# A column mean over 8192 x 8192: reordering the last six tiles and splitting them differently between VectorE and TensorE

## Chip, cores, metric

The kernel runs on one core of one Trainium2 chip. The metric is device time in microseconds (us), lower is better. "Span" is the time from the first to the last instruction in the profile; it is about 2 us shorter than the time of the same run.

Names used below: PE is TensorE, DVE is VectorE, ACT is ScalarE, SP is SyncE. SP and ACT only issue DMAs here, except for two small copies on ACT at the end. "Tile t" is rows 128t to 128t+127 of the input (128 x 8192 floats, 4 MB). "Block b" is columns 512b to 512b+511. The two DMA queues are also called rings. A load has "landed" when its data are in the buffer. The "granted clock" is the share of PE's full clock that it was given.

## The reference

```python
def setup_inputs():
    return {"x": np.random.randn(8192, 8192).astype(np.float32)}

def reference(x):
    return np.mean(x, axis=0)
```

The kernel reads 268 MB and writes 32 KB. So it cannot be faster than the input can be loaded.

## The kernel before

64 tiles come in over two DMA queues (even tiles from SP, odd ones from ACT) into four buffers (tile 0 goes straight into `acc`). DVE adds each tile to an accumulator `acc` of 128 x 8192. At the end PE sums over the 128 partitions: a matmul of one block with a 128 x 16 matrix, whose only nonzero column holds 1/8192, adds the block's column sums to one row of a PSUM tile. `psA` holds blocks 0 to 13, `psB` blocks 14 and 15. Since such a matmul accumulates, PE can also take a block of a tile directly, without DVE. The text calls such blocks "raw".

```python
    def mm(src, b, ps, row, start, stop):
        nc.tensor.matmul(out=ps[:], lhsT=w16[:, 16 - row : 32 - row],
            rhs=src[:, b * BLK : (b + 1) * BLK], start=start, stop=stop)
    # ... mmA: a row of psA; mmB: a row of psB; raws(src): blocks 13, 14, 15 of src

    for t0 in range(0, 56, 2):
        # ... load tiles t0 and t0+1 whole, one on each queue; DVE adds 8192 columns of each

    for t0 in (56, 58, 60):
        # ... load both tiles whole; at 56: mmA(acc, 13), mmB(acc, 14), mmB(acc, 15)
        # DVE adds columns 0:6656 (blocks 0 to 12) of each; then raws() of each

    dve_units = [(g * 1024, (g + 1) * 1024) for g in range(5)] + [
        (b * BLK, (b + 1) * BLK) for b in (10, 11, 12)
    ]
    # ... tile 62 on SP: raw columns first, then dve_units
    for c0, c1 in dve_units:                       # tile 63 on ACT: raw blocks LAST
        nc.scalar.dma_start(out=pbuf[63][:, c0:c1], in_=x[63 * P : 64 * P, c0:c1])
    for b in PE_B:                                 # (13, 14, 15)
        c0, c1 = b * BLK, (b + 1) * BLK
        nc.scalar.dma_start(out=pbuf[63][:, c0:c1], in_=x[63 * P : 64 * P, c0:c1])

    raws(pbuf[62])
    done_blk = 0
    for c0, c1 in dve_units:
        order = (63, 62) if c1 - c0 == 1024 else (62, 63)
        for t in order:
            nc.vector.tensor_add(out=acc[:, c0:c1], in0=acc[:, c0:c1], in1=pbuf[t][:, c0:c1])
        while (done_blk + 1) * BLK <= c1:
            mmA(acc, done_blk)
            done_blk += 1
    mmA(pbuf[63], 13, stop=True)
    mmB(pbuf[63], 14)
    mmB(pbuf[63], 15, stop=True)
    # ... ACT copies psA and psB to SBUF, two DMAs write the output
```

The order of instructions on PE is not the order of the text here; a scheduler sets it when the program is built. In the trace of this kernel the two `psB` matmuls of tile 63, last in the text, start at 626.14 us, ahead of the 13 matmuls of sums, which run from 629.4 on.

Of the kernel before, what the change touches and what calls it, by code (L numbers as in the profile page):

```python
# [1 line left out]

# [4 lines left out]


@with_exitstack
def kernel(  # L10
    ctx: ExitStack,
    tc: tile.TileContext,
    x: bass.AP,
    out: bass.AP,
):
    nc = tc.nc
    P = nc.NUM_PARTITIONS
    R, C = x.shape
    assert R % P == 0
    n_tiles = R // P  # L20
    fp32 = mybir.dt.float32

    BLK = 512
    n_blk = C // BLK
    assert n_blk <= 16 and C % BLK == 0

    special = n_tiles == 64 and C == 8192
    N_STREAM_BUFS = 4

    acc_pool = ctx.enter_context(tc.tile_pool(name="acc", bufs=1))  # L30
    acc = acc_pool.tile([P, C], fp32, tag="acc", name="acc")

    const_pool = ctx.enter_context(tc.tile_pool(name="const", bufs=1))
    w16 = const_pool.tile([P, 48], fp32, tag="w16", name="w16")
    res = const_pool.tile([16, BLK], fp32, tag="res", name="res")
    res2 = const_pool.tile([2, BLK], fp32, tag="res2", name="res2")

    stream_pool = ctx.enter_context(tc.tile_pool(name="stream", bufs=N_STREAM_BUFS))

    psum_pool = ctx.enter_context(tc.tile_pool(name="psum", bufs=1, space=bass.MemoryType.PSUM))  # L40
    psA = psum_pool.tile([16, BLK], fp32, tag="psA", name="psA")
    psB = psum_pool.tile([16, BLK], fp32, tag="psB", name="psB")

    rings = [nc.sync, nc.scalar]
    out2d = out.rearrange("(a b) -> a b", b=BLK)

    rings[0].dma_start(out=acc[:], in_=x[0:P, :])  # L47
    nc.vector.memset(w16[:], 0.0)  # L48
    nc.vector.memset(w16[:, 16:17], 1.0 / R)  # L49

    def mm(src, b, ps, row, start, stop):
        nc.tensor.matmul(  # L52
            out=ps[:],
            lhsT=w16[:, 16 - row : 32 - row],
            rhs=src[:, b * BLK : (b + 1) * BLK],
            start=start,
            stop=stop,
        )

    if not special:  # L60
        for t0 in range(0, n_tiles, 2):
            pair = [t for t in (t0, t0 + 1) if 0 < t < n_tiles]
            bufs = {}
            for t in pair:
                bufs[t] = stream_pool.tile([P, C], fp32, tag="xt", name=f"x_t{t}")
                rings[t % 2].dma_start(out=bufs[t][:], in_=x[t * P : (t + 1) * P, :])
            for t in pair:
                nc.vector.tensor_add(out=acc[:], in0=acc[:], in1=bufs[t][:])
        for b in range(n_blk):
            mm(acc, b, psA, row=b, start=(b == 0), stop=(b == n_blk - 1))  # L70
        nc.scalar.copy(out=res[:n_blk], in_=psA[:n_blk])
        nc.scalar.dma_start(out=out2d, in_=res[:n_blk])
        return

    PE_B = (13, 14, 15)
    D1 = PE_B[0] * BLK

    psA_started = [False]
    psB_started = [False]

    def mmA(src, b, stop=False):
        mm(src, b, psA, row=b, start=not psA_started[0], stop=stop)
        psA_started[0] = True

    def mmB(src, b, stop=False):
        mm(src, b, psB, row=b - 14, start=not psB_started[0], stop=stop)
        psB_started[0] = True

    def raws(src, stop=False):
        mmA(src, 13)  # L90
        mmB(src, 14)
        mmB(src, 15, stop=stop)

    for t0 in range(0, 56, 2):
        pair = [t for t in (t0, t0 + 1) if t > 0]
        bufs = {}
        for t in pair:
            bufs[t] = stream_pool.tile([P, C], fp32, tag="xt", name=f"x_t{t}")
            rings[t % 2].dma_start(out=bufs[t][:], in_=x[t * P : (t + 1) * P, :])
        for t in pair:  # L100
            nc.vector.tensor_add(out=acc[:], in0=acc[:], in1=bufs[t][:])  # L101

    for t0 in (56, 58, 60):
        bufs = {}
        for t in (t0, t0 + 1):
            bufs[t] = stream_pool.tile([P, C], fp32, tag="xt", name=f"x_t{t}")
            rings[t % 2].dma_start(out=bufs[t][:], in_=x[t * P : (t + 1) * P, :])  # L107
        if t0 == 56:
            mmA(acc, 13)
            mmB(acc, 14)  # L110
            mmB(acc, 15)
        for t in (t0, t0 + 1):
            nc.vector.tensor_add(  # L113
                out=acc[:, 0:D1], in0=acc[:, 0:D1], in1=bufs[t][:, 0:D1]
            )
        for t in (t0, t0 + 1):
            raws(bufs[t])

    dve_units = [(g * 1024, (g + 1) * 1024) for g in range(5)] + [
        (b * BLK, (b + 1) * BLK) for b in (10, 11, 12)  # L120
    ]
    pbuf = {}
    for t in (62, 63):
        pbuf[t] = stream_pool.tile([P, C], fp32, tag="xt", name=f"x_t{t}")
    nc.sync.dma_start(out=pbuf[62][:, D1:C], in_=x[62 * P : 63 * P, D1:C])
    for c0, c1 in dve_units:
        nc.sync.dma_start(out=pbuf[62][:, c0:c1], in_=x[62 * P : 63 * P, c0:c1])
    for c0, c1 in dve_units:
        nc.scalar.dma_start(out=pbuf[63][:, c0:c1], in_=x[63 * P : 64 * P, c0:c1])  # L129
    for b in PE_B:  # L130
        c0, c1 = b * BLK, (b + 1) * BLK
        nc.scalar.dma_start(out=pbuf[63][:, c0:c1], in_=x[63 * P : 64 * P, c0:c1])  # L132

    raws(pbuf[62])

    done_blk = 0
    for c0, c1 in dve_units:
        order = (63, 62) if c1 - c0 == 1024 else (62, 63)
        for t in order:
            nc.vector.tensor_add(  # L140
                out=acc[:, c0:c1], in0=acc[:, c0:c1], in1=pbuf[t][:, c0:c1]
            )
        while (done_blk + 1) * BLK <= c1:
            mmA(acc, done_blk)
            done_blk += 1
    assert done_blk == 13

    mmA(pbuf[63], 13, stop=True)
    mmB(pbuf[63], 14)
    mmB(pbuf[63], 15, stop=True)  # L150

    nc.scalar.copy(out=res[0:14], in_=psA[0:14])  # L152
    nc.sync.dma_start(out=out2d[0:14], in_=res[0:14])
    nc.scalar.copy(out=res2[0:2], in_=psB[0:2])  # L154
    nc.scalar.dma_start(out=out2d[14:16], in_=res2[0:2])


# [1 line left out]
_INS = ['x']  # L159
_OUTS = [((8192,), 'float32')]  # L160


# [23 lines left out]
```

## Time and profile before

| what | before |
|---|---|
| time, median of 13 runs | 647.78 us (647.07 to 648.64) |
| span of the profiled run | 645.4 us |
| HBM rate over the span | 416 GB/s |
| DVE busy | 83% |
| PE busy | 7% |

The part of the page that cuts the span into 40 slices of 16.1 us, kernel before. The digits are busy tenths; PEclk is the granted PE clock in tenths of full speed.

```profile
DVE  0538998888898888898888998888998888987693
...
PEclk9999999999999999999999999999999999997669
DMA  9999999999999999999999999999999999999970
GB/s 390 422 433 445 422 422 443 435 422 433 445 422 424 443 433 422 433 445 422 425 441 433 424 433 441 424 426 441 433 424 435 439 424 424 443 433 425 411 304 2
```

DMA is full from start to slice 38. DVE follows it, at about nine tenths. There is nothing to win in the first 600 us except a faster DMA. What can be won is the end: the last slice has an almost empty DMA, and the one before it is down to 304 GB/s.

Two windows of the same trace. The columns are: busy us (and instructions) of PE, PEld, DVE, ACT, POOL; granted clock; DMA share; GB/s.

```profile
120.00:480.00 360.00, 0.00 (x0) 0.00 (x0) 322.52 (x38) 0.00 (x0) 0.00 (x0) 1.00 1.00 432
610.00:620.00 10.00, 4.71 (x11) 0.87 (x9) 9.93 (x3) 0.00 (x0) 0.00 (x0) 0.95 1.03 405
```

In the steady part the tiles come in rows of 32 KB at 432 GB/s. From 606 us on they come in pieces with rows of 2 to 6 KB, at 405 GB/s between 610 and 620 us.

The end of the chain of waits, which is the work that ended last, followed back from step to step to what released it (start us, duration us, what):

```profile
619.55 6.55 DMA x_t<-in_x_dram
...
626.14 3.46 PE psB L52 x4
629.60 12.03 PE psA L52 x28
...
641.66 0.57 ACT res L152
```

The last of tile 63 lands at 626.1 to 626.7 us (semaphore events of the trace). Then PE multiplies for 15.5 us, 16 matmuls, before the copy and the output. Each matmul is two instructions in this trace (the reason why "x28" is 14 matmuls), 0.43 us apart each at full clock: 0.86 us per block. The granted clock was 0.50 from 619.1 to 629.3 us here, and the instructions issued in that time were 0.85 us apart; that is why 16 matmuls took 15.5 us and not 16 x 0.86 = 13.8.

DVE in the same stretch (timeline; in brackets the idle time before, and what ended it; a line with several adds is named after the first, so "x16" is ten adds of 1024 columns and six of 512):

```profile
585.43 14.22 DVE L113 TENSOR_TENSOR acc<-acc,x_t 128x6656 f32<-128x6656 f32 x2 [5.21 <-DMA x_t<-in_x_dram]
604.87 14.22 DVE L113 TENSOR_TENSOR acc<-acc,x_t 128x6656 f32<-128x6656 f32 x2 [5.22 <-DMA x_t<-in_x_dram]
619.12 15.05 DVE L140 TENSOR_TENSOR acc<-acc,x_t 128x1024 f32<-128x1024 f32 x16
```

DVE has no gap from 604.87 to 634.17. So two things end late: PE at 641.63, because its queue waited for the last landing, and DVE at 634.2, 8 us after the last data.

### The profile page before, as it was taken

The numbers are of one execution on the slowest core, as the hardware profiler recorded it, in microseconds if no ns is written. First come the engines' busy times: TensorE is split into PE (matmuls) and PEld (weight loads), VectorE is DVE, ScalarE is ACT, GpSimd is POOL, SyncE is SP. The second block draws the span as 40 slices with busy tenths as digits, with TensorE's granted clock in tenths as the row PEclk, the third lists the DMA queues.
The fourth block names the chain that finished last, engine by engine and source line by source line (L and its number), as shares of the span: only waits on it lengthen the run. The fifth ranks groups of instructions, "written<-read, shape, count | busy, mean of one in ns | idle before, by whom it ended". The sixth has DMA issues, their size and how long they took to land.

```text
span 645.4 us, 503 instructions
## 1 busy us (share of the span) xinstructions
PE 42.0 (7%) x80; PEld 8.2 (1%) x80; DVE 535.8 (83%) x79; ACT 2.4 (0%) x3; POOL 0.2 (0%) x4
## 2 busy tenths in 40 slices
PE   0000000000000000000000000000000000054527
PEld 0000000000000000000000000000000000010101
DVE  0538998888898888898888998888998888987693
ACT  0000000000000000000000000000000000000000
POOL 0000000000000000000000000000000000000000
PEclk9999999999999999999999999999999999997669
DMA  9999999999999999999999999999999999999970
GB/s 390 422 433 445 422 422 443 435 422 433 445 422 424 443 433 422 433 445 422 425 441 433 424 433 441 424 426 441 433 424 435 439 424 424 443 433 425 411 304 2
DMA packets 11842, 268.49 MB, mean 416 GB/s; under 512 B 1328, under 2 KB 1328, under 8 KB 3904
## 3 DMA queue, kind: packets, MB, share of 16 engines
q1 hardware_dynamic: 5788, 134.25, 48.5%
q10 hardware_dynamic: 6052, 134.22, 48.5%
q14 instruction: 2, 0.02, 0.0%
HBM read 268.44 MB, written 0.03 MB: 416 GB/s over the span
## 4 chain that ended last, share of the span: by engine, by line
DMA 74%; DVE 22%; PE 2%; another core or an unknown queue 0%; issue 0%; ACTq 0%; ACT 0%; SPq 0%; DVEq 0%
DMA x_t<-in_x_dram 74%; DVE acc L101 20%; DVE acc L113 2%; PE psA L52 2%; PE psB L52 1%; ACTq L129 0%; ACT res L152 0%; ACTq L132 0%; SPq L47 0%; DVEq L101 0%; ACTq L107 0%; DVEq L113 0%
## 5 line engine op out<-in xcount | busy, mean ns | idle before, releaser
L101 DVE TENSOR_TENSOR acc<-acc,x_t 128x8192 f32<-128x8192 f32 x55 | 478.1, 8692 | 84.9 <-DMA x_t<-in_x_dram 84.0
L113 DVE TENSOR_TENSOR acc<-acc,x_t 128x6656 f32<-128x6656 f32 x6 | 42.6, 7092 | 12.6 <-DMA x_t<-in_x_dram 12.4
L52 PE MATMUL psA<-acc,w 128*16 128x512 f32 x28 | 13.2, 625 | 564.0 <-DVE acc L101 564.0
L52 PE MATMUL psB<-x_t,w 128*16 128x512 f32 x32 | 18.5, 708 | 11.4 <-DMA x_t<-in_x_dram 11.4
L140 DVE TENSOR_TENSOR acc<-acc,x_t 128x1024 f32<-128x1024 f32 (+1 forms) x16 | 15.1, 1019 | 0.0
L52 PE MATMUL psA<-x_t,w 128*16 128x512 f32 x16 | 9.9, 706 | 24.2 <-DMA x_t<-in_x_dram 24.2
L52 PEld LDWEIGHTS psA<-acc,w 128*16 128x16 f32 x28 | 2.7, 100 | 573.3 <-DVE acc L101 564.0
L52 PEld LDWEIGHTS psB<-x_t,w 128*16 128x16 f32 x32 | 3.5, 112 | 25.8 <-DMA x_t<-in_x_dram 13.1
L154 ACT ACT_TABLE_LOAD x1 | 1.3, 1283 | 621.8 <-DMA x_t<-in_x_dram 621.8
L52 PE MATMUL psB<-acc,w 128*16 128x512 f32 x4 | 3.0, 887 | 0.0
L52 PEld LDWEIGHTS psA<-x_t,w 128*16 128x16 f32 x16 | 1.4, 99 | 30.5 <-DMA x_t<-in_x_dram 26.0
L48 DVE MEMSET w<- 128x48 f32 x1 | 0.1, 98 | 0.8 <-PEq L170 0.8
L52 PEld LDWEIGHTS psB<-acc,w 128*16 128x16 f32 x4 | 0.6, 151 | 2.8 <-issue 2.8
L152 ACT COPY res<-psA 14x512 f32<-14x512 f32 x1 | 0.6, 574 | 11.4 <-PE psA L52 11.4
L154 ACT COPY res<-psB 2x512 f32<-2x512 f32 x1 | 0.6, 574 | 6.5 <-PE psB L52 6.5
L49 DVE MEMSET w<- 128x1 f32 x1 | 0.1, 59 | 0.1
L170 POOL MEMSET const-bfloat16-1.0<- 128x1 bf16 x1 | 0.1, 101 | 0.0
L170 POOL MEMSET const-uint8-127<- 128x1 uint8 x1 | 0.1, 101 | 0.0
L170 POOL MEMSET const-float32-0.0<- 128x1 f32 x1 | 0.1, 98 | 0.2 <-issue 0.2
L170 POOL MEMSET const-float32-1.0<- 128x1 f32 x1 | 0.1, 98 | 0.0
## 6 DMA issues: line engine op xcount, KB each, us to landing
x_t<-in_x_dram ACTq DMA_DIRECT2D x31, 4096.0 KB, 24.5
x_t<-in_x_dram SPq DMA_DIRECT2D x30, 4096.0 KB, 30.1
acc<-in_x_dram SPq DMA_DIRECT2D x1, 4096.0 KB, 21.7
x_t<-in_x_dram SPq DMA_DIRECT2D x5, 512.0 KB, 19.1
x_t<-in_x_dram ACTq DMA_DIRECT2D x5, 512.0 KB, 6.7
x_t<-in_x_dram ACTq DMA_DIRECT2D x6, 256.0 KB, 6.2
x_t<-in_x_dram SPq DMA_DIRECT2D x1, 768.0 KB, 16.4
x_t<-in_x_dram SPq DMA_DIRECT2D x3, 256.0 KB, 6.8
```

What stands on the lines that cost most here:

```text
L48: nc.vector.memset(w16[:], 0.0)
L49: nc.vector.memset(w16[:, 16:17], 1.0 / R)
L52: nc.tensor.matmul(out=ps[:], lhsT=w16[:, 16 - row : 32 - row], rhs=src[:, b * BLK : (b + 1) * BLK], start=start, stop=stop,)
L101: nc.vector.tensor_add(out=acc[:], in0=acc[:], in1=bufs[t][:])
L113: nc.vector.tensor_add(out=acc[:, 0:D1], in0=acc[:, 0:D1], in1=bufs[t][:, 0:D1])
L140: nc.vector.tensor_add(out=acc[:, c0:c1], in0=acc[:, c0:c1], in1=pbuf[t][:, c0:c1])
L152: nc.scalar.copy(out=res[0:14], in_=psA[0:14])
L154: nc.scalar.copy(out=res2[0:2], in_=psB[0:2])
L170: nc = _bacc.Bacc("TRN2", target_bir_lowering=False, num_devices=1)
```

## The change

It means to shorten the end. PE's instruction order is pinned to the text (`manual_schedule`). The raw blocks of tiles 62 and 63 are loaded and multiplied first, so that after the last add only a matmul of a summed block is left. PE takes six raw blocks instead of three of tiles 58 to 61. Tiles 60 and 61 come in pieces. The core of the diff, with cuts:

```diff
-    for t0 in range(0, 56, 2):
+    for t0 in range(0, 58, 2):                 # two more full tiles for DVE
 ...
-    for t0 in (56, 58, 60):
-        ... whole loads; DVE columns 0:6656, PE blocks 13, 14, 15
+    with tc.manual_schedule(engines={mybir.EngineType.PE}):
+        mmB(acc, 14)
+        mmB(acc, 15)
+        PE_LO = 10
+        D1 = PE_LO * BLK
+        ... tiles 58, 59: whole loads; DVE columns 0:5120, PE blocks 10 to 15
+        dve_units_a = [(g * 1024, (g + 1) * 1024) for g in range(5)]
+        for t in (60, 61):
+            bufs[t] = new_buf(t)
+            rings[t % 2].dma_start(out=bufs[t][:, D1:C], in_=x[t * P : (t + 1) * P, D1:C])
+            for c0, c1 in dve_units_a:
+                rings[t % 2].dma_start(
+                    out=bufs[t][:, c0:c1], in_=x[t * P : (t + 1) * P, c0:c1])
+        ... DVE adds the five units of 60 and 61, PE blocks 10 to 15
-    ... tile 62: raw first; tile 63: raw last; psA of sums, then psA, psB, psB of tile 63
+        raw_units = [(7168, 8192)]
+        tail_units = dve_units_a + [(5120, 6144), (6144, 6656), (6656, 7168)]
+        for c0, c1 in raw_units + tail_units:
+            for t in (62, 63):
+                rings[t % 2].dma_start(
+                    out=bufs[t][:, c0:c1], in_=x[t * P : (t + 1) * P, c0:c1])
+        for c0, c1 in raw_units:
+            for t in (62, 63):
+                for b in range(c0 // BLK, c1 // BLK):
+                    mm_raw(bufs[t], b, stop=(t == 63 and b == 15))
+        for c0, c1 in tail_units:
+            for t in (62, 63):
+                nc.vector.tensor_add(
+                    out=acc[:, c0:c1], in0=acc[:, c0:c1], in1=bufs[t][:, c0:c1])
+            for b in range(c0 // BLK, c1 // BLK):
+                mmA(acc, b, stop=(c1 == tail_units[-1][1] and b == c1 // BLK - 1))
```

More of the change, by code (lines that the diff above doesn't have):

```diff
@@ L58, in mm, with new_buf @@
         )
+    def new_buf(t):
+        return stream_pool.tile([P, C], fp32, tag="xt", name=f"x_t{t}")
     if not special:
@@ L64 @@
             for t in pair:
-                bufs[t] = stream_pool.tile([P, C], fp32, tag="xt", name=f"x_t{t}")
+                bufs[t] = new_buf(t)
                 rings[t % 2].dma_start(out=bufs[t][:], in_=x[t * P : (t + 1) * P, :])
@@ L73 @@
         return
-    PE_B = (13, 14, 15)
-    D1 = PE_B[0] * BLK
     psA_started = [False]
@@ L87, in mmB, with mm_raw @@
         psB_started[0] = True
-    def raws(src, stop=False):
-        mmA(src, 13)
-        mmB(src, 14)
-        mmB(src, 15, stop=stop)
-    for t0 in range(0, 56, 2):
+    def mm_raw(src, b, stop=False):
+        if b >= 14:
+            mmB(src, b, stop=stop)
+        else:
+            mmA(src, b, stop=stop)
+    bufs = {}
+    for t0 in range(0, 58, 2):
         pair = [t for t in (t0, t0 + 1) if t > 0]
-        bufs = {}
         for t in pair:
-            bufs[t] = stream_pool.tile([P, C], fp32, tag="xt", name=f"x_t{t}")
+            bufs[t] = new_buf(t)
             rings[t % 2].dma_start(out=bufs[t][:], in_=x[t * P : (t + 1) * P, :])
@@ L101 @@
             nc.vector.tensor_add(out=acc[:], in0=acc[:], in1=bufs[t][:])
-    for t0 in (56, 58, 60):
-        bufs = {}
-        for t in (t0, t0 + 1):
-            bufs[t] = stream_pool.tile([P, C], fp32, tag="xt", name=f"x_t{t}")
-            rings[t % 2].dma_start(out=bufs[t][:], in_=x[t * P : (t + 1) * P, :])
-        if t0 == 56:
-            mmA(acc, 13)
-            mmB(acc, 14)
-            mmB(acc, 15)
-        for t in (t0, t0 + 1):
-            nc.vector.tensor_add(
-                out=acc[:, 0:D1], in0=acc[:, 0:D1], in1=bufs[t][:, 0:D1]
-            )
-        for t in (t0, t0 + 1):
-            raws(bufs[t])
@@ L119 @@
-    dve_units = [(g * 1024, (g + 1) * 1024) for g in range(5)] + [
-        (b * BLK, (b + 1) * BLK) for b in (10, 11, 12)
-    ]
-    pbuf = {}
-    for t in (62, 63):
-        pbuf[t] = stream_pool.tile([P, C], fp32, tag="xt", name=f"x_t{t}")
-    nc.sync.dma_start(out=pbuf[62][:, D1:C], in_=x[62 * P : 63 * P, D1:C])
-    for c0, c1 in dve_units:
-        nc.sync.dma_start(out=pbuf[62][:, c0:c1], in_=x[62 * P : 63 * P, c0:c1])
-    for c0, c1 in dve_units:
-        nc.scalar.dma_start(out=pbuf[63][:, c0:c1], in_=x[63 * P : 64 * P, c0:c1])
@@ L130 @@
-    for b in PE_B:
-        c0, c1 = b * BLK, (b + 1) * BLK
-        nc.scalar.dma_start(out=pbuf[63][:, c0:c1], in_=x[63 * P : 64 * P, c0:c1])
-    raws(pbuf[62])
-    done_blk = 0
-    for c0, c1 in dve_units:
-        order = (63, 62) if c1 - c0 == 1024 else (62, 63)
-        for t in order:
-            nc.vector.tensor_add(
-                out=acc[:, c0:c1], in0=acc[:, c0:c1], in1=pbuf[t][:, c0:c1]
-            )
-        while (done_blk + 1) * BLK <= c1:
-            mmA(acc, done_blk)
-            done_blk += 1
@@ L146 @@
-    assert done_blk == 13
-    mmA(pbuf[63], 13, stop=True)
-    mmB(pbuf[63], 14)
-    mmB(pbuf[63], 15, stop=True)
-    nc.scalar.copy(out=res[0:14], in_=psA[0:14])
-    nc.sync.dma_start(out=out2d[0:14], in_=res[0:14])
-    nc.scalar.copy(out=res2[0:2], in_=psB[0:2])
-    nc.scalar.dma_start(out=out2d[14:16], in_=res2[0:2])
+    with tc.manual_schedule(engines={mybir.EngineType.PE}):
[3 more added lines that the diff above has]
+        D1 = PE_LO * BLK
+        for t in (58, 59):
+            bufs[t] = new_buf(t)
+            rings[t % 2].dma_start(out=bufs[t][:], in_=x[t * P : (t + 1) * P, :])
+        for t in (58, 59):
+            nc.vector.tensor_add(out=acc[:, 0:D1], in0=acc[:, 0:D1], in1=bufs[t][:, 0:D1])
+        for t in (58, 59):
+            for b in range(PE_LO, 16):
+                mm_raw(bufs[t], b)
+        dve_units_a = [(g * 1024, (g + 1) * 1024) for g in range(5)]
+        for t in (60, 61):
+            bufs[t] = new_buf(t)
+            rings[t % 2].dma_start(out=bufs[t][:, D1:C], in_=x[t * P : (t + 1) * P, D1:C])
+            for c0, c1 in dve_units_a:
+                rings[t % 2].dma_start(
+                    out=bufs[t][:, c0:c1], in_=x[t * P : (t + 1) * P, c0:c1]
+                )
+        for c0, c1 in dve_units_a:
+            for t in (60, 61):
+                nc.vector.tensor_add(
+                    out=acc[:, c0:c1], in0=acc[:, c0:c1], in1=bufs[t][:, c0:c1]
+                )
+        for t in (60, 61):
+            for b in range(PE_LO, 16):
+                mm_raw(bufs[t], b)
+        raw_units = [(7168, 8192)]
+        tail_units = dve_units_a + [(5120, 6144), (6144, 6656), (6656, 7168)]
+        for t in (62, 63):
+            bufs[t] = new_buf(t)
+        for c0, c1 in raw_units + tail_units:
+            for t in (62, 63):
+                rings[t % 2].dma_start(
+                    out=bufs[t][:, c0:c1], in_=x[t * P : (t + 1) * P, c0:c1]
+                )
+        for c0, c1 in raw_units:
[3 more added lines that the diff above has]
+        for c0, c1 in tail_units:
+            for t in (62, 63):
+                nc.vector.tensor_add(
+                    out=acc[:, c0:c1], in0=acc[:, c0:c1], in1=bufs[t][:, c0:c1]
+                )
+            for b in range(c0 // BLK, c1 // BLK):
+                mmA(acc, b, stop=(c1 == tail_units[-1][1] and b == c1 // BLK - 1))
+        nc.scalar.copy(out=res2[0:2], in_=psB[0:2])
+        nc.scalar.dma_start(out=out2d[14:16], in_=res2[0:2])
+        nc.scalar.copy(out=res[0:14], in_=psA[0:14])
+        nc.sync.dma_start(out=out2d[0:14], in_=res[0:14])
```

## The prediction

> **What bounds it now.** The page: DMA is nine tenths busy or more in nearly every slice; 416 GB/s over a 645.4 us span. The chain of waits repeats every 38.85 us per four tiles (16.8 MB, 432 GB/s); DVE adds take 8.69 us per 128x8192 tile, 17.4 of every 19.4 us. So up to about 605 us DMA binds, and the change leaves that alone. The last pieces of tile 63 land at 626.1 to 626.7. What follows is a 19 us tail.
>
> In the chain, PE starts psB at 626.14 (3.46 us), then psA (12.03 us), to 641.63; the psA copy (0.57 us) and the output DMA end the span 3.8 us later. PE's instruction order has tile 63's two psB matmuls ahead of all psA matmuls of finished blocks. They wait for the last landings, and 13 psA matmuls that could have started near 622 queue behind. DVE ends at 634.2, without a gap from 604.87 (2 x 7.09 us for tiles 60, 61, then 15.05 us).
>
> **What the change does.**
> - PE order pinned, raw blocks of 62/63 loaded and multiplied first: psA matmuls run as units finish, one matmul remains after the last add. Removes up to 12 us of tail.
> - Six blocks instead of three go to PE for tiles 58 to 61: DVE saves 4 x 1.6 us (8.69 less 7.09, per 1536 columns); tiles 56, 57 become full adds (+2 x 1.6), tiles 62/63 have one block more (+1.0). PE gets some 10 us more work, off the chain.
> - Tiles 60, 61 come in pieces, so their adds start near 596 instead of 605. This relieves DVE at the end.
> - Cost: 4 KB rows move at 405 GB/s against 432 (table of windows); 5.2 MB more of them is about 0.8 us. More DMAs wait for an earlier one's semaphore; two rings with work queued should hide that.
> - DVE's order has tile 62's first unit before tile 61's last, so DVE idles till about 610.
>
> **Estimate.** Laying landings (432/405 GB/s, two rings sharing) and adds (1.13 us per 1024 columns, 0.63 per 512) side by side: last landing 626.5 to 627.3, hardly changed; DVE then has two units of backlog and ends near 629; the last four matmuls take 0.86 us each at full clock, so PE ends near 630.7 against 641.63. 647.5 - 10.9 = 636.6 us, 1.7% less. Even with only one add and one matmul after the last landing it would be near 633.
>
> **Clock.** [...] granted 0.50 until 608.9, then 1.00. At half clock a matmul is 1.71 us. I expect PE busy without a break from about 608 to 618[...]; half clock there would add 3.5 us.
>
> Predicted 636.5 us, 8 in 10 between 633.0 and 640.5. Faster by over 2%: 0.22; within 2%: 0.77; slower by over 2%: 0.01.
>
> **What would show it.** Right: last landing within 1 us of 626.5; last add near 629; chain ending DMA, DVE adds, one to four psA matmuls, copy; psB copy long before; slices up to 36 as before. Wrong: more than 4 matmuls piled up after the last add; DVE ending after 631; last landing after 628.
>
> **What would make it wrong.** A dry ring (issues held by semaphores) in 600 to 626, delaying the last landing; DVE's fixed order stalling on late units; half clock at the end. Faster if the smaller pieces overlap better and DVE keeps pace.

Full clock for the last four matmuls was the assumption. 641.63 - 630.7 = 10.9, and 647.5 - 10.9 = 636.6 us, with the four matmuls at the 0.86 us each that the trace shows at granted clock 1.00. "Half clock there" means at the last four matmuls: 4 x (1.71 - 0.86) = 3.4 us by these figures. The waits for "an earlier one's semaphore" are those of the trace before: of the 14 loads issued from 600 us on, 10 were issued 0.02 to 0.05 us after the earlier DMA on the same semaphore had landed. That two rings would hide more of them was an estimate.

## The result

| | before | after |
|---|---|---|
| median, runs | 647.78 us, 13 | 637.82 us, 8 |
| range | 647.07 to 648.64 | 637.64 to 638.1 |
| span of the profiled run | 645.4 | 635.9 |
| last landing | 626.7 | 627.5 |
| last add of DVE ends | 634.2 | 630.6 |
| last matmul of PE ends | 641.6 | 632.3 |
| mean granted PE clock | 0.974 | 0.999 |

The ratio is 0.9844 (95% interval 0.9834 to 0.9853): 10 us, 1.6%.

The slices after, of 15.9 us each:

```profile
DVE  0538998888988888988889888899888898888966
...
PEclk9999999999999999999999999999999999999999
DMA  9999999999999999999999999999999999999994
GB/s 385 439 429 429 429 429 429 429 433 437 439 437 431 429 429 429 429 429 429 435 437 435 437 431 429 429 429 429 429 429 437 437 435 437 431 429 416 410 409 156
```

Up to slice 36 DMA and DVE are about as busy as before. The end of the chain of waits after:

```profile
611.94 7.99 DMA x_t<-in_x_dram
...
620.02 2.44 DVE acc L151 x3
...
623.43 0.98 DVE acc L151
...
624.57 1.77 DVE acc L151 x2
...
627.44 1.23 DVE acc L151
...
628.72 3.62 PE psA L52 x8
...
632.36 0.57 ACT res L158
```

Where before showed 15.5 us of matmuls after the last landing, there are now adds up to 630.6 us and the last eight PE instructions (four matmuls, 3.6 us). DVE's timeline after:

```profile
585.64 11.02 DVE L114 TENSOR_TENSOR acc<-acc,x_t 128x5120 f32<-128x5120 f32 x2 [2.01 <-DMA x_t<-in_x_dram]
596.69 1.22 DVE L129 TENSOR_TENSOR acc<-acc,x_t 128x1024 f32<-128x1024 f32 x1
...
603.18 2.36 DVE L129 TENSOR_TENSOR acc<-acc,x_t 128x1024 f32<-128x1024 f32 x2 [0.19 <-DMA x_t<-in_x_dram]
607.52 2.36 DVE L129 TENSOR_TENSOR acc<-acc,x_t 128x1024 f32<-128x1024 f32 x2 [1.98 <-DMA x_t<-in_x_dram]
...
614.90 4.63 DVE L151 TENSOR_TENSOR acc<-acc,x_t 128x1024 f32<-128x1024 f32 x4 [2.75 <-DMA x_t<-in_x_dram]
620.02 10.57 DVE L151 TENSOR_TENSOR acc<-acc,x_t 128x1024 f32<-128x1024 f32 x11 [0.49 <-DMA x_t<-in_x_dram]
```

DVE starts on tile 60 at 596.7, not at 604.9. Yet it then waits for landings, about 5 us in all between 600 and 615, and it still ends 3 us after the last landing. The two windows after:

```profile
120.00:480.00 360.00, 0.00 (x0) 0.00 (x0) 322.31 (x38) 0.00 (x0) 0.00 (x0) 1.00 1.00 432
610.00:620.00 10.00, 4.19 (x9) 0.72 (x10) 6.78 (x6) 0.00 (x0) 0.00 (x0) 1.00 1.02 409
```

The steady part is the same to the digit. At the end it is 409 GB/s in 4 KB rows.

### The profile page after: what moved, and what is told of

The parts are those of the page before. It is cut to its first block, busy times and chain, and to the rows that moved or that the text cites. A ratio compares the mean times of both kernels' runs of the same rounds, so it can differ in the third digit from the quotient of the medians.

```text
span 635.9 us, 537 instructions
## 1 busy us (share of the span) xinstructions
PE 40.5 (6%) x88; PEld 8.1 (1%) x88; DVE 534.6 (84%) x87; ACT 2.4 (0%) x3; POOL 0.2 (0%) x4
## 4 chain that ended last, share of the span: by engine, by line
DMA 78%; DVE 20%; issue 1%; PE 1%; ACT 0%; SPq 0%; DVEq 0%
DMA x_t<-in_x_dram 78%; DVE acc L102 19%; DVE acc L151 1%; PE psA L52 1%; ACT res L158 0%; SPq L47 0%; DVEq L102 0%; DVEq L151 0%
## 5 line engine op out<-in xcount | busy, mean ns | idle before, releaser
L102 DVE TENSOR_TENSOR acc<-acc,x_t 128x8192 f32<-128x8192 f32 x57 | 495.5, 8692 | 87.1 <-DMA x_t<-in_x_dram 64.5
L151 DVE TENSOR_TENSOR acc<-acc,x_t 128x1024 f32<-128x1024 f32 (+1 forms) x16 | 16.4, 1087 | 3.3 <-DMA x_t<-in_x_dram 3.2
L52 PE MATMUL psA<-x_t,w 128*16 128x512 f32 x32 | 14.4, 592 | 0.0
L129 DVE TENSOR_TENSOR acc<-acc,x_t 128x1024 f32<-128x1024 f32 x10 | 11.8, 1222 | 2.6 <-DMA x_t<-in_x_dram 2.6
L114 DVE TENSOR_TENSOR acc<-acc,x_t 128x5120 f32<-128x5120 f32 x2 | 11.0, 5491 | 2.0 <-DMA x_t<-in_x_dram 2.0
L52 PE MATMUL psB<-x_t,w 128*16 128x512 f32 x24 | 11.1, 593 | 2.8 <-DMA x_t<-in_x_dram 2.8
L156 ACT ACT_TABLE_LOAD x1 | 1.3, 1283 | 622.6 <-DMA x_t<-in_x_dram 622.6
L52 PEld LDWEIGHTS psA<-x_t,w 128*16 128x16 f32 x32 | 3.2, 99 | 11.4 <-issue 10.6
L52 PEld LDWEIGHTS psA<-acc,w 128*16 128x16 f32 x28 | 2.3, 96 | 15.8 <-DVE acc L151 10.9
L52 PEld LDWEIGHTS psB<-x_t,w 128*16 128x16 f32 x24 | 2.2, 97 | 11.0 <-issue 7.3
```

The costliest lines, as they stand in the source:

```text
L102: nc.vector.tensor_add(out=acc[:], in0=acc[:], in1=bufs[t][:])
L114: nc.vector.tensor_add(out=acc[:, 0:D1], in0=acc[:, 0:D1], in1=bufs[t][:, 0:D1])
L156: nc.scalar.copy(out=res2[0:2], in_=psB[0:2])
```

## The experiments

The twelve runs used below stand in one table first. Times are medians; ratios are to the kernel before in the same rounds. The three event columns come from the profiled execution of each.

| run | time us | ratio [95%] | last landing | last add ends | PE ends |
|---|---|---|---|---|---|
| (after) | 637.82 | 0.9844 [0.9834, 0.9853] | 627.5 | 630.6 | 632.3 |
| pin_only | 643.90 | 0.9941 [0.9926, 0.9956] | 626.8 | 634.3 | 638.6 |
| raw_first | 641.10 | 0.9891 [0.9875, 0.9907] | 626.8 | 634.4 | 635.9 |
| no_pin | 639.67 | 0.9872 [0.9855, 0.9888] | 627.5 | 632.5 | 634.3 |
| whole_6061 | 638.95 | 0.9861 [0.9846, 0.9875] | 626.7 | 632.2 | 634.1 |
| lo13 | 639.64 | 0.9876 [0.9861, 0.9891] | 627.6 | 633.0 | 634.8 |
| pin_dve | 637.73 | 0.9847 [0.9832, 0.9861] | 627.6 | 631.2 | 632.3 |
| dve_skew | 636.96 | 0.9834 [0.9820, 0.9849] | 627.6 | 629.6 | 631.5 |
| best3_dve | 637.00 | 0.9836 [0.9820, 0.9853] | 627.0 | 630.8 | 632.0 |
| best4 | 636.09 | 0.9821 [0.9808, 0.9834] | 627.4 | 630.1 | 631.5 |
| best5 | 638.30 | 0.9858 [0.9843, 0.9873] | 626.8 | 629.9 | 632.8 |
| best6 | 636.87 | 0.9832 [0.9819, 0.9845] | 627.1 | 630.1 | 631.5 |
| after_again | 637.83 | 0.9846 [0.9833, 0.9860] | 627.6 | 630.7 | 632.4 |

### 1. PE's order alone: pin_only

```diff
 (kernel before)
+    with tc.manual_schedule(engines={mybir.EngineType.PE}):
         ... everything from tile 56 to tile 63's matmuls, unchanged
```

> The kernel before with nothing changed but PE's instruction order, pinned to the order of the text: the 13 psA matmuls of summed blocks come before tile 63's raw blocks. Theory 1 (the tail of before was PE's queue head waiting for tile 63, with DVE as the next limit): DVE still ends near 634.2 us, then one psA matmul and the three raw ones of tile 63 (4 x 0.86 us) remain, PE ends near 637.6 instead of 641.6, time about 643.5 us. Theory 2 (the gain came from relieving DVE, PE's order alone is worth nothing because DVE ends at 634 anyway): about 647.8 us, unchanged.

It took 643.90 us, so 0.59% less: 3.8 us of the 10 come from the order of PE's queue and nothing else. Theory 2 is out. The end of the chain of waits of this run:

```profile
622.78 14.12 PE psA L52 x28
636.90 1.73 PE psB L52 x4
```

PE starts on sums at 622.8 instead of standing at the head of a queue that waits for tile 63. It ended 1 us later than expected. It runs without a break from 622.8 to 638.6, and its granted clock was 0.50 until 626.7. So PE, not DVE's last add, held the end here.

### 2. Tile 63's raw blocks first as well: raw_first

```diff
 (pin_only)
+        nc.scalar.dma_start(out=pbuf[63][:, D1:C], in_=x[63 * P : 64 * P, D1:C])
         for c0, c1 in dve_units:
             nc.scalar.dma_start(out=pbuf[63][:, c0:c1], ...)
-        for b in PE_B:
-            ... three loads of 256 KB at the end
         raws(pbuf[62])
+        raws(pbuf[63], stop=True)
 ...
-        mmA(pbuf[63], 13, stop=True)
-        mmB(pbuf[63], 14)
-        mmB(pbuf[63], 15, stop=True)
```

> As pin_only, and tile 63's raw blocks are loaded first (one DMA of 768 KB, as tile 62 has it) and multiplied before the psA matmuls of summed blocks. DVE work and its start are those of before. Theory 1: only one matmul is left after the last add at about 634.2, PE ends near 635.1, time about 641.0 us: two thirds of the change's gain without touching the split of work between DVE and PE. Theory 2: about 647 us.

641.10 us, as theory 1 had it. This kernel has DVE's work of before, to the microsecond (last add at 634.4), and PE's work of before. It gives 1.09% of the change's 1.56%, which is 7 of the 10 us. The chain's last link:

```profile
622.87 13.03 PE psA L52 x26
```

The 13 matmuls of sums take 13.0 us, ending 1.5 us after the last add. The granted clock was 0.50 from 622.6 to 626.0 us, so PE had a little to catch up here too.

### 3. Without the pin: no_pin

```diff
 (the changed kernel)
-    with tc.manual_schedule(engines={mybir.EngineType.PE}):
+    if True:
```

> The changed kernel without the pinned PE order. The built program has the same order of the last 18 matmuls, only the first few of tiles 58 and 59 move. Theory A (loading and multiplying the raw blocks first is what takes the wait out of PE's queue; the pin is not needed): 637.8 us, as with it, within 0.3 us. Theory B (the pin is what does it): 641 us or more.

639.67 us: between the two theories, and so neither is right as put. PE's last 18 matmuls keep their order without the pin, as theory A says. Still it is 1.8 us slower. The last landing is the same (627.5 in both), but DVE ends 1.9 us later, because it waits in the middle:

```profile
597.96 2.36 DVE L129 TENSOR_TENSOR acc<-acc,x_t 128x1024 f32<-128x1024 f32 x2 [0.31 <-DMA x_t<-in_x_dram]
603.35 4.63 DVE L129 TENSOR_TENSOR acc<-acc,x_t 128x1024 f32<-128x1024 f32 x4 [3.03 <-DMA x_t<-in_x_dram]
...
616.41 4.63 DVE L151 TENSOR_TENSOR acc<-acc,x_t 128x1024 f32<-128x1024 f32 x4 [3.08 <-DMA x_t<-in_x_dram]
621.95 10.57 DVE L151 TENSOR_TENSOR acc<-acc,x_t 128x1024 f32<-128x1024 f32 x11 [0.92 <-DMA x_t<-in_x_dram]
```

The trace shows why. In the traces of the kernel before and of the changed kernel, the landings of all DMAs (84 and 92) are reported on the same eight semaphores (counters). In none of the 160 cases where a DMA followed another on its semaphore (76 and 84) was it issued before that one had landed; the shortest time between was 0.02 us. Without the pin the scheduler emits the DMAs in a slightly different order, so they get other semaphores. From the issue and landing events, for the five DVE pieces of tile 61 (us):

```
                    piece 0   piece 1   piece 2   piece 3   piece 4
after   issued       587.25    593.74    596.58    600.59    603.17
after   landed       596.89    600.42    603.37    607.43    609.69
no_pin  issued       587.65    596.35    599.23    600.52    600.89
no_pin  landed       596.97    603.26    606.07    608.61    611.17
```

In the changed kernel piece 1 shares its semaphore with tile 60's raw part, which landed at 593.71: it is issued at 593.74. Without the pin it shares one with tile 60's first unit, which landed at 596.33: it is issued at 596.35. It lands 2.8 us later and DVE stands still for it. That wait alone does not reach the end, because the changed kernel waits further on, until 614.90 for tile 63's first unit. In no_pin this same wait lasts until 616.41, and 0.4 us more is lost at 621.95: together the 1.9 us. Tile 63's first unit lands at 616.31 against 614.81, although it was issued a little earlier (606.09 against 606.82). Its queue was behind: tile 61's last piece, ahead of it, landed 1.5 us later than in the changed kernel. So the pin's worth in the changed kernel is not PE's order at the end. The two kernels differ otherwise only in the first few matmuls of tiles 58 and 59. That the semaphores make the whole 1.8 us is read from these traces, not tried by itself.

### 4. Tiles 60 and 61 whole: whole_6061

```diff
 (the changed kernel)
-            rings[t % 2].dma_start(out=bufs[t][:, D1:C], in_=x[t * P : (t + 1) * P, D1:C])
-            for c0, c1 in dve_units_a:
-                rings[t % 2].dma_start(
-                    out=bufs[t][:, c0:c1], in_=x[t * P : (t + 1) * P, c0:c1])
+            rings[t % 2].dma_start(out=bufs[t][:], in_=x[t * P : (t + 1) * P, :])
```

> The changed kernel, but tiles 60 and 61 are loaded in one DMA each, as before, with their adds still in 1024-column units. Theory C (their pieces relieve DVE by letting its adds start near 596 instead of 605): DVE runs without a gap from about 605, 10 units and 16 units take 27.1 us, it ends near 632.1, PE near 633.8, time about 639.3 us. Theory D (the end is set by the last landing, and smaller rows cost 0.8 us of DMA time): last landing near 626.7 and time about 637.0 us, faster than the changed kernel.

638.95 us, theory C. Both halves of the trade are visible. The larger rows bring the last landing 0.9 us forward (626.65 against 627.52), as the 432 and 405 GB/s had said. But DVE cannot start before 604.7, and then has 27.5 us of adds without a gap:

```profile
604.73 11.44 DVE L125 TENSOR_TENSOR acc<-acc,x_t 128x1024 f32<-128x1024 f32 x10 [8.80 <-DMA x_t<-in_x_dram]
616.09 16.11 DVE L147 TENSOR_TENSOR acc<-acc,x_t 128x1024 f32<-128x1024 f32 x16
```

It ends at 632.2, and the net is 1.1 us lost. When DVE can start is worth more here than the DMA rate.

### 5. The wider share for PE: lo13

```diff
 (the changed kernel)
-        PE_LO = 10
+        PE_LO = 13
-        dve_units_a = [(g * 1024, (g + 1) * 1024) for g in range(5)]
+        dve_units_a = [(g * 1024, (g + 1) * 1024) for g in range(6)] + [(6144, 6656)]
-        tail_units = dve_units_a + [(5120, 6144), (6144, 6656), (6656, 7168)]
+        tail_units = dve_units_a + [(6656, 7168)]
```

> The changed kernel, but PE takes three blocks of tiles 58 to 61, as before, not six: 6.4 us more of DVE adds. Theory E (the wider share for PE buys DVE little, as DVE idles about 5.8 us between 596 and 615 anyway, waiting for landings): last add 0.5 to 1.5 us later, time 638.3 to 639.5 us. Theory F (the wider share is what relieves DVE): last add up to 6 us later, time about 643 us.

639.64 us: nearer to E than to F, but 0.1 us outside the range. DVE's last add comes 2.4 us later, not 6.4 and not 0.5 to 1.5:

```profile
585.46 14.22 DVE L114 TENSOR_TENSOR acc<-acc,x_t 128x6656 f32<-128x6656 f32 x2 [2.02 <-DMA x_t<-in_x_dram]
599.72 14.32 DVE L129 TENSOR_TENSOR acc<-acc,x_t 128x1024 f32<-128x1024 f32 x13
...
617.90 15.12 DVE L151 TENSOR_TENSOR acc<-acc,x_t 128x1024 f32<-128x1024 f32 x15 [2.13 <-DMA x_t<-in_x_dram]
```

Of 6.4 us more adds, 4.0 fill time that DVE would have waited in; 2.4 come out at the end. This run also cuts tiles 60 and 61 into two more pieces each, so its landings move as well; the two effects were not separated.

### 6. DVE's order: pin_dve and dve_skew

```diff
 (the changed kernel)                                      pin_dve
-    with tc.manual_schedule(engines={mybir.EngineType.PE}):
+    with tc.manual_schedule(engines={mybir.EngineType.PE, mybir.EngineType.DVE}):
```

```diff
 (pin_dve)                                                 dve_skew
-        for c0, c1 in tail_units:
-            for t in (62, 63):
-                ... add unit of t
+        steps = [(62, 0)]
+        for i in range(n):                     # n = len(tail_units)
+            if i + 1 < n:
+                steps.append((62, i + 1))
+            steps.append((63, i))
+        for t, i in steps:
+            ... add unit i of t; after tile 63's, its matmuls
```

> The changed kernel with DVE's order pinned to the text as well: tile 61's last unit before tile 62's first, and units of 62 and 63 strictly in turn. Each DMA keeps the semaphore it had, so the landings should stay. Theory P (my prediction: the scheduler's DVE order costs time by stalling on late units): DVE's last add earlier by 1 us or more, time 636.8 us or less. Theory Q (from 614.8 us, where tile 63's first unit lands, DVE has 15.7 us of adds left in any order that has no unit of tile 62 done before): no change, 637.8 us within 0.5.

> As pin_dve, but DVE takes tile 62's units one ahead of tile 63's, as they land (62's pieces land 3 to 5 us before 63's of the same columns in the changed kernel). One more 1024-column add fits before 614.8 us. Theory Q: last add 1.1 us earlier, near 629.5, time about 636.7 us. Theory P: same as pin_dve.

The strict order changes nothing (637.73 us). Taking tile 62 one unit ahead gives 0.8 us (636.96), and the last add moves from 631.2 to 629.6. The lines that differ, pin_dve and then dve_skew:

```profile
611.07 1.22 DVE L151 TENSOR_TENSOR acc<-acc,x_t 128x1024 f32<-128x1024 f32 x1
614.95 2.36 DVE L151 TENSOR_TENSOR acc<-acc,x_t 128x1024 f32<-128x1024 f32 x2 [2.66 <-DMA x_t<-in_x_dram]
...
620.06 11.16 DVE L151 TENSOR_TENSOR acc<-acc,x_t 128x1024 f32<-128x1024 f32 x11 [0.19 <-DMA x_t<-in_x_dram]
```

```profile
611.09 2.35 DVE L157 TENSOR_TENSOR acc<-acc,x_t 128x1024 f32<-128x1024 f32 x2
614.98 2.36 DVE L157 TENSOR_TENSOR acc<-acc,x_t 128x1024 f32<-128x1024 f32 x2 [1.54 <-DMA x_t<-in_x_dram]
...
620.10 9.53 DVE L157 TENSOR_TENSOR acc<-acc,x_t 128x1024 f32<-128x1024 f32 x10 [0.19 <-DMA x_t<-in_x_dram]
```

In pin_dve one add of 1024 columns is done before the wait that ends at 614.95; in dve_skew there are two. From there on DVE runs almost without a gap, so each add moved ahead comes off the end. That is theory Q. My prediction had blamed the scheduler's order of tiles 61, 62 and 63 for DVE's wait; pin_dve shows that this order is not the cause. DVE waits for tile 63's pieces. In the changed kernel they land 1.4 to 5.4 us after tile 62's pieces of the same columns (first unit 614.81 against 609.37). ACT issues six of the eight units within 0.03 us of the landing of an earlier DMA with the same semaphore, and the other two right behind one of these. That these late issues make the lag is read from the trace; no run takes them away alone.

### 7. Attempts at a version that beats both

All four pin DVE's order. They load tiles 60 and 61 in fewer, larger pieces, and use smaller units at the very end.

```diff
 best3_dve: tiles 60, 61 as columns (0, 4096), (4096, 8192), PE blocks 13 to 15 of them
            tail units 2048, 2048, 1024, 512 x 4; strict order 62, 63
 best4:     tiles 60, 61 as (0, 3072), (6144, 8192), (3072, 6144), PE blocks 12 to 15 of them
            tail units 1024 x 5, 512 x 4; tile 62 one unit ahead
 best5:     as best4, tail units 1024, 1024, 2048, 1024, 512 x 4
 best6:     tiles 60, 61 as best3_dve; tail as best4
```

> A version meant to beat both: tiles 60 and 61 in two DMAs of 4096 columns each (fewer DMAs, so none waits for an earlier one's semaphore, and 16 KB rows), three blocks of them for PE, tiles 62 and 63 in units of 2048, 2048, 1024 and four of 512 columns after the raw ones, DVE's order pinned. If semaphore holds and DVE's backlog are what is left of the tail: DVE adds from 597 on, last landing near 626.3, last add near 627.3, PE one matmul later, 628.5 to 629, time about 634.5 us. If PE is short of time once its clock has dropped in the wait before 605 us: 636 us or more.

> What best3_dve lacked: its first units of tiles 62 and 63 were 2048 columns wide and landed only at 613.5 us, so DVE idled 2.5 us and ended at 630.8. Here the units are five of 1024 and four of 512 columns, DVE takes tile 62 one unit ahead, and tiles 60 and 61 come in three pieces each (3072 columns for DVE, the four blocks for PE, 3072 for DVE). If DVE's late start was all: adds of 60 and 61 end near 611.5, then 16.3 us of adds with little waiting, last add near 628.2, PE near 629.2, time near 635.0 us. If landings of 63 lag as in the changed kernel (its issues held by semaphores): 636.5 us or more.

> As best4 with one unit of 2048 columns in place of the third and fourth of 1024: fewer DMAs and semaphores, 8 KB rows there, but coarser landings. Time near 635.0 us as best4 if neither matters by more than 0.5 us.

> best4 with tiles 60 and 61 in two DMAs of 4096 columns each and three blocks of them for PE, as in best3_dve. In best4 tile 63's first loads were held until 606.4 us, because they share a semaphore with tile 60's last piece; here they share it with tile 60's first one, landed near 595.6. If that hold was best4's remaining loss: 63's raw and first unit issued near 597, DVE without a gap from 605 on, last add near 628, time near 635.0 us. If not: 636 us, as best4.

> The changed kernel, unaltered, on the same chip as best6 for a fair comparison: ratio 0.984 to before, as on record.

For the dropped clock in best3_dve's expectation, the trace before shows this: granted 0.50 from 595.2 to 608.9 us, with PE standing still until 604.8.

The changed kernel, run again beside best6: 0.9846. None of the four reached the figure hoped for. best4 has the lowest median, 636.09 us, ratio 0.9821 to before, 1.7 us below the changed kernel by the medians, 1.5 us by the ratios; its interval overlaps those of dve_skew, best3_dve and best6. It still did not reach the 635.0 that I had expected. DVE ends at 630.1, not 628.2:

```profile
606.28 6.75 DVE L128 TENSOR_TENSOR acc<-acc,x_t 128x3072 f32<-128x3072 f32 x2 [2.64 <-DMA x_t<-in_x_dram]
...
615.78 14.31 DVE L158 TENSOR_TENSOR acc<-acc,x_t 128x1024 f32<-128x1024 f32 x16 [0.48 <-DMA x_t<-in_x_dram]
```

Most of this is the wait for tile 60's last piece, which had been issued at 575.99 and landed at 606.26: the adds of tiles 60 and 61 end at 613.0, not 611.5. Tile 63's first load was again issued late, at 606.36, just after tile 60's last piece had landed on the same semaphore (606.26), but that cost DVE only the 0.48 us before 615.78. And PE works without a gap at the end:

```profile
621.74 1.89 PE L52 MATMUL psA<-acc,w 128*16 128x512 f32 x4 [0.38 <-DVE acc L158]
624.01 7.42 PE L52 MATMUL psA<-acc,w 128*16 128x512 f32 x16 [0.38 <-DVE acc L158]
```

From 624.0 to 631.4 it is never idle, so here PE has become the limit as well.

best6 took away that late issue: tile 63's raw part was issued at 597.4 and landed at 609.3. It came out no faster (636.87). DVE had one block more of tiles 60 and 61 to add, and after these adds it waited four times, about 2.5 us in all. The longest wait, 0.98 us, was for a later unit of tile 63 that was issued late instead (issued 616.68, landed 622.86). In best3_dve DVE waited for its first unit of 2048 columns until 613.56. In best5, 2.2 us slower than best4, PE had 10 matmuls without a gap at the end:

```profile
624.01 8.76 PE L52 MATMUL psA<-acc,w 128*16 128x512 f32 x20 [1.45 <-DVE acc L158]
```

Its granted clock had been 0.50 up to 618.4 us, but that was made good: at full clock PE waited 1.45 us for DVE before 624.01. DVE's add of the 2048-column unit ended at 623.96 and left PE more than it could work off by DVE's last add (629.9). So the trace points to the coarser unit, not the clock. In sum: the late issues moved about with the DMA list (606.36 in best4, 616.68 in best6). In these four kernels PE still ends 1.1 to 2.9 us after DVE's last add.

## Why the prediction was right

It said 636.5 us (633.0 to 640.5) and "within 2%"; the time was 637.82. Point by point:

- **What bounds it, and that the first 600 us stay:** right. 432 GB/s between 120 and 480 us before and after.
- **The order of PE's queue is the main cost:** right and shown. Order alone gives 3.8 us, order with the raw blocks first 7 of the 10 us, with DVE's work untouched (experiments 1 and 2). About 1.7 of the 15.5 us was half clock (0.50 until 629.3); pin_only and raw_first start their sums at half clock too (0.50 until 626.7 and 626.0), so their gains do not come from that. That the *pin* brings it in the changed kernel is not right: without it PE's order at the end is the same (experiment 3). The pin is still worth 1.8 us there, by way of the landings, which the prediction did not name. To that extent the closeness of the number is luck; without the pin it would have been 639.67, still in the range.
- **"This relieves DVE at the end", of the pieces of tiles 60 and 61:** right, worth 1.1 us net (experiment 4). But the prediction tied the relief to the pieces; it listed the wider share for PE as adds saved and gave it no worth at the end. Without it the time is about 2 us longer, partly perhaps because of the two more pieces for each of tiles 60 and 61 (experiment 5).
- **Smaller rows cost about 0.8 us:** right. 0.87 us of last landing, measured in experiment 4.
- **Last landing 626.5 to 627.3:** 627.5, off by 0.2.
- **Last add near 629:** 630.6. This is the term that was mis-sized, and it makes all of the 1.3 us that the prediction was short. The step was "two rings with work queued should hide that": the rings never ran dry (409 GB/s), so the last landing did not suffer, but *which* data came first did change. Tile 63's units lagged tile 62's by 1.4 to 5.4 us, DVE stood still for 2.75 us until the first of them was there (614.90), and it had four adds (3.1 us) left when the last piece landed, where the prediction's own figures leave about 2 us. That the semaphores make the lag is read from the issue and landing times and not shown by a run of its own.
- **DVE's order as a risk:** half right. The order of tile 62's first unit and tile 61's last is the wrong suspect: pin_dve changed nothing. But a fixed order did stall on a late unit, tile 63's first, and dve_skew, which changes DVE's order alone, gains 0.8 us.
- **Four matmuls after the last adds, at full clock:** right. 3.6 us for four, from 628.72; granted clock 1.00 from 587.0 to 634.8. In after_again, the same kernel, it was 0.50 from 617.3 to 624.1 us. It was back at 1.00 before the last four matmuls, and the time was the same (637.83).

## What to carry to other kernels

When a kernel is limited by loading, look at what stands behind the last landing, and at the head of each engine's queue at that moment: here one instruction that waited for the last data until 626.14 us held back 13 matmuls that could have run, and reordering alone gave 3.8 us (experiment 1). Let the last data need the shortest work: load first what needs the longest path, or only one engine, and keep for the end what is one add and one matmul. Count semaphores when you cut loads into pieces: the DMA rate stayed the same here (409 GB/s from 596 to 605 us with and without the pin) while a single piece came 2.8 us later (experiment 3), and the engine that takes the pieces in order waited for it. Then ask which wait ends last: an earlier one can be made good before the end, as in experiments 3 and 7.
